# One chunk instead of two by seven products in the last third of a gated MLP, and a last chunk that issues its matmuls ahead of its additions and stores

## The chip, the core and the metric

The kernel runs on one core of one Trainium2 chip. The metric is the device time of one execution in microseconds (us). Five engines work side by side, each in the order of its own instruction list: TensorE (PE, matmuls; its weight loads, PEld, overlap them), VectorE (DVE), ScalarE (ACT), GpSimd (POOL) and SyncE (SP, which here issues the transfers). Matmuls add up in PSUM banks of 128 partitions by 512 fp32 numbers.

## What is computed

One hybrid decoder layer on 256 tokens of width 2048: a norm, one input projection into attention heads and a pooling mixer, an output projection, and then the part that matters here, a gated MLP with a residual:

```python
def conv_ffn(h, w_up, conv_w, conv_b, w_down):
    u = h @ w_up
    ...
    gate, val = jnp.split(y, 2, axis=-1)
    return (jax.nn.silu(gate) * val) @ w_down
...
x = x + conv_ffn(rms_norm(x, ffn_norm_g[l]), w_up[l], conv_w[l], conv_b[l], w_down[l])
```

The hidden width is 5632, that is 44 blocks of 128 rows of `w_down`. All is fp32.

## The kernel before

**Three matmuls for one product.** Each fp32 operand is split into a rounded high part and a low part. A product of two operands is then high·high + low·high + high·low: three matmuls (`triple`, lines 703–706, and the loops over `((0, 0), (1, 0), (0, 1))`). For the weights ScalarE makes the high part `wh` (line 124) and VectorE the low part `wl` (line 129), both 128x1024.

**Units and chunks.** The whole weight stream is cut into units of 128x1024; two units are one chunk, loaded by one 1024 KB transfer into one of four `raw` buffers (line 105). A buffer is given back and the load of the chunk four later issued when the low part of the chunk's second unit has been made (`release`, lines 160–164). There are seven `wh` and six `wl` buffers.

**The order.** A list `steps` holds one entry per unit; the loop in lines 830–853 walks it. In turn `u` it writes the split of units `u+6` (high) and `u+5` (low), the matmuls of unit `u`, and whatever was hung onto that step. So the order of every engine's list comes from this loop; an engine that waits holds all that stands behind it.

**The last product.** The hidden width is worked off in three thirds of 8, 8 and 6 block pairs (`THIRDS`, line 57). Each third first makes its hidden activations (`gate`, `value`) and then multiplies them with its rows of `w_down` in two passes, `down_pair(bp, ...)` with `bp` 0 and 1, one for each half of the 2048 output columns. A pass over a third has as many chunks as block pairs. The output of a pass lies in four PSUM banks, `bank(t, b)`: token tile `t` (128 tokens) by column half `b` (512); the two banks of one `t` are one tile, `ps_down`.

A chunk is a 2x2 block of weights against a 2x2 block of activations (two row blocks by two column halves, two row blocks by two token tiles):

- The plain form (`quad`, lines 744–752) makes eight block products, 24 matmuls, 12 for each unit.
- The form by seven products (`quad_sums`, lines 727–742) makes 21 matmuls, 12 for the first unit and 9 for the second. It needs sums of activations (`token_sums`, lines 690–701, on GpSimd, ScalarE, VectorE) and sums of weights: `seven_sums` (lines 139–145) writes on VectorE a 128x512 low part (line 150) and three subtractions (lines 143–145), and `seven_high`/`seven_low` a further 128x1024 part `s4` (lines 148 and 157).

`MIXED` (line 58) says which chunks of a third take the form by seven: `8: (0, 4)` for the first two thirds, `6: (0, 3)` for the last. Three of the seven products gather in PSUM tiles of their own (`ps_p`, in code `aux`, `p5`, `p7`). When the last chunk of that form in a pass is through, five pieces of work, `add_part(0)` to `add_part(4)`, add these to the residual `x2` (lines 769–783): pieces 0 and 2 are a copy by ScalarE (line 774) and a VectorE addition in PSUM (line 775), pieces 1, 3 and 4 VectorE additions of 128x1024 into `x2` (lines 777, 780, 783). They are hung onto the steps by

```python
s_end = 2 * mixed[-1] + 1
rest = 2 * nq - 1 - s_end
...
if at == s_end + 1 + n * (rest - 1) // 5:
```

With six chunks and `(0, 3)` that gives the steps 8, 8, 9, 9 and 10 of a pass's 12 (0 to 11).

**The end of a pass.** After the last step `close` (lines 785–791) adds the four banks to `x2`, 128x1024 for each `t`, and stores it if this is the last third. The very last pass has no `close`: its last chunk goes through `last_quad` (lines 754–767). For each bank in turn, the last one in two halves of 256 columns, it issues the chunk's six matmuls, then the addition to `x2` (line 766), then the store (line 767).

Of the kernel before, what the change touches and what calls it, by code (L numbers as in the profile page):

```python
# [28 lines left out]
OP = mybir.AluOpType  # L29
# [5 lines left out]
NT = S // P  # L35
# [19 lines left out]
OK = (0, 2, 4, 6, 12, 14, 8, 10)  # L55
V_TILES = [((k, 0), (k, 1)) for k in range(KT - 2)] + [((KT - 2, b), (KT - 1, b)) for b in range(2)]
THIRDS = ((0, 8), (8, 16), (16, 22))
MIXED = {8: (0, 4), 6: (0, 3)}


def bucket(n):
# [9 lines left out]
def layer(ctx: ExitStack, tc: tile.TileContext, xT, xtok, wts, par, rel_d, ident_d, icnt_d, out):  # L71
    nc = tc.nc
# [24 lines left out]
    raws, wparts, shift, late = {}, {}, {}, {}  # L97
# [444 lines left out]
    def after(u, f):  # L542

        hooks.append((u, f))
# [22 lines left out]
    for b in range(2):  # L567
# [4 lines left out]
        for j in range(4):  # L572
            h, u = 4 * b + j, at + 2 * j
# [134 lines left out]
    def down_pair(bp, nq, final):  # L708


        box, runs, mixed = {}, [], MIXED[nq]
        s_end = 2 * mixed[-1] + 1
        rest = 2 * nq - 1 - s_end

        def hid(k, t):
            return [late["hid"][:, k, a, t * P:(t + 1) * P] for a in range(2)]
# [4 lines left out]
        def bank(t, b):  # L721
            return box["tok"][t][:, b, :]

        def part(w, c):
            return [p[:, 512 * c:512 * (c + 1)] for p in w]
# [27 lines left out]

        def last_quad(us, j):
            ws = [wparts.pop(u) for u in us]
            for t in range(NT):
                for b in range(2):
                    cs = (slice(0, 512),) if t * b == 0 else (slice(0, 256), slice(256, 512))
                    for c in cs:
                        for h, w in enumerate(ws):  # L760
                            w = [p[:, c] for p in part(w, b if h == 0 else 1 - b)]
                            for n, (a, i) in enumerate(((0, 0), (1, 0), (0, 1))):
                                nc.tensor.matmul(bank(t, b)[:, c], hid(2 * j + h, t)[a], w[i], start=False,  # L763
                                                 stop=(h == 1 and n == 2), skip_group_check=True)
                        x2 = late["x2"][:, t, (2 * bp + b) * 512:(2 * bp + b + 1) * 512][:, c]
                        nc.vector.tensor_tensor(x2, bank(t, b)[:, c], x2, op=OP.add)
                        nc.sync.dma_start(out[:, t, (2 * bp + b) * 512:(2 * bp + b + 1) * 512][:, c], x2)

        def add_part(n):
            x2 = late["x2"][:, :, 1024 * bp:1024 * (bp + 1)]  # L770
# [23 lines left out]
        for j in range(nq):  # L794
            for h in range(2):
                at = 2 * j + h

                def run(u, j=j, h=h, at=at):
                    if j in mixed:
                        quad_sums(u, j, h)  # L800
                    elif end and j == nq - 1:
                        if h == 1:
                            last_quad((u - 1, u), j)
                    else:
                        quad(u, j, h)
                run.seven = j in mixed and h == 0
                acts = [run]
                for n in range(5):
                    if at == s_end + 1 + n * (rest - 1) // 5:
                        acts.append(lambda n=n: add_part(n))  # L810
                if at == 2 * nq - 1 and not end:
                    acts.append(lambda: close(0))
                runs.append(acts)
        return runs

    for n, (g0, g1) in enumerate(THIRDS):
        after(len(steps), lambda nq=g1 - g0: late.__setitem__("mixed", MIXED[nq]))
        for g in range(g0, g1):
# [7 lines left out]
    n = len(steps)  # L826
# [94 lines left out]
```

## Time and profile before

| | |
|---|---|
| median of 3 runs | 1027.93 us (1027.73 to 1028.13) |
| the profiled execution's own time | 1027.94 us |
| its span, first to last instruction | 1025.8 us |
| TensorE busy | 1015.5 us, 99% of the span |
| VectorE busy | 771.5 us, 75% |
| ScalarE busy | 545.9 us, 53% |

Busy time is summed over the span. A row of the timeline gives the start, the time, the engine, the line, what is written and read and how many were merged, and in brackets how long the engine had been idle and who ended that. A row of the chain of waits is a piece of the chain that ended last. A row of a window gives the length of the window and the busy time of each engine in it with its count of instructions.

### The profile page before, as it was taken

What the parts mean: (1) busy time and instruction counts of PE and PEld (TensorE: products, weight loads), DVE (VectorE), ACT (ScalarE), POOL (GpSimd) and SP (SyncE); (2) the same over time, 40 slices, a digit from 0 to 9 for tenths busy, and PEclk for the clock granted to TensorE, in tenths of its full rate; (3) what the DMA queues carried; (4) which work ended last, traced back from release to release, by engine and by line L of the source; (5) the groups of instructions that cost most, each with busy time, mean ns of one, the idle gap of its engine ahead of it and who ended that gap; (6) DMA issues with size and microseconds to landing.
All of it is one profiled execution on the core that took longest, in us unless ns stands there. A gap on an engine that the chain in (4) does not pass through costs nothing.

```text
span 1025.8 us, 13519 instructions
## 1 busy us (share of the span) xinstructions
PE 1015.5 (99%) x5280; PEld 869.7 (85%) x5280; DVE 771.5 (75%) x968; ACT 545.9 (53%) x734; POOL 63.4 (6%) x78
## 2 busy tenths in 40 slices
PE   9999999999999999999999999999999999999987
PEld 8888888888888888888888888888888888888776
DVE  6966667874667877878977687777898767778994
ACT  6744554565445655555644455555554446555650
POOL 0420005600000000000000000000000000000000
PEclk9999999999999999999999999999999999999999
DMA  9775454485454564454565364554465644545451
GB/s 334 273 279 176 172 169 161 165 306 186 164 205 149 200 215 176 165 195 183 207 241 200 124 234 177 207 186 182 165 246 187 224 165 164 211 180 185 172 197 41
DMA packets 30607, 199.18 MB, mean 194 GB/s; under 512 B 3576, under 2 KB 4472, under 8 KB 7760
## 3 DMA queue, kind: packets, MB, share of 16 engines
q1 hardware_dynamic: 29968, 196.89, 52.9%
q0 software_dynamic: 576, 1.44, 0.6%
q8 instruction: 41, 0.67, 0.3%
q14 instruction: 22, 0.18, 0.0%
HBM read 195.83 MB, written 2.49 MB: 193 GB/s over the span
## 4 chain that ended last, share of the span: by engine, by line
PE 96%; DVE 3%; issue 1%; ACT 0%; DVEq 0%; ACTq 0%
PE ps_feat L185 34%; PE ps_feat L187 17%; PE ps_tok L172 17%; PE ps_down L750 14%; PE ps_v L179 4%; PE ps_p L706 3%; PE ps_down L706 2%; DVE wl L129 1%; PE ps_down L763 1%; PE ps_pool L194 1%; PE ps_s L400 1%; PE ps_start L247 0%; PE ps_T L387 0%; PE ps_x2T L615 0%; PE ps_av L433 0%
## 5 line engine op out<-in xcount | busy, mean ns | idle before, releaser
L129 DVE TENSOR_TENSOR wl<-raw,wh 128x1024 fp32r<-128x1024 f32 x358 | 435.7, 1252 | 75.5 <-PE ps_tok L172 27.7
L185 PE MATMUL ps_feat<-x2h,wh 128*128 128x512 f32 x1408 | 488.6, 392 | 0.0
L124 ACT ACTIVATE wh<-raw 128x1024 fp32r<-128x1024 f32 x358 | 361.7, 1051 | 159.1 <-DVE raw L143 54.5
L187 PE MATMUL ps_feat<-x2h,wl 128*128 128x256 f32 x1408 | 393.6, 280 | 0.0
L185 PEld LDWEIGHTS ps_feat<-x2h,wh 128*128 128x128 f32 x1408 | 264.3, 188 | 58.4
L187 PEld LDWEIGHTS ps_feat<-x2h,wl 128*128 128x128 f32 x1408 | 264.3, 188 | 0.1
L750 PE MATMUL ps_down<-wh,hid 128*128 128x512 f32 x496 | 122.5, 389 | 0.0
L750 PEld LDWEIGHTS ps_down<-wh,hid 128*128 128x128 f32 x496 | 93.1, 188 | 19.3
L667 ACT ACTIVATE y<-u,pv 128x256 f32<-128x256 f32 x88 | 48.2, 594 | 71.5 <-DVE u L662 71.5
L172 PE MATMUL ps_tok<-wh,xh 128*128 128x512 f32 x256 | 70.1, 396 | 0.0
L172 PE MATMUL ps_tok<-wh,cat 128*128 128x512 f32 x256 | 68.8, 390 | 0.0
L750 PE MATMUL ps_down<-wl,hid 128*128 128x512 f32 x248 | 66.3, 389 | 0.0
L668 DVE SCALAR_TENSOR_TENSOR y<-u,pv,y 128x256 f32<-128x256 f32 x88 | 42.4, 482 | 29.6 <-ACT y L667 29.6
L450 DVE TENSOR_TENSOR fs<-ps_feat,fs 128x512 f32<-128x512 f32 x44 | 30.4, 690 | 36.0 <-ACT fs L449 35.9
L172 PEld LDWEIGHTS ps_tok<-wh,cat 128*128 128x128 f32 x256 | 47.6, 188 | 9.6
L172 PEld LDWEIGHTS ps_tok<-wh,xh 128*128 128x128 f32 x256 | 47.5, 188 | 9.5
L750 PEld LDWEIGHTS ps_down<-wl,hid 128*128 128x128 f32 x248 | 46.6, 188 | 9.7
L699 POOL TENSOR_TENSOR s<-y 128x128 f32<-128x128 f32 x12 | 7.3, 612 | 693.9 <-DVE y L684 693.9
L449 ACT ACTIVATE fs<-ps_feat 128x512 f32<-128x512 f32 x44 | 26.1, 594 | 41.6 <-PE ps_feat L187 41.4
L185 PE MATMUL ps_feat<-xh,wh 128*128 128x512 f32 x128 | 46.2, 402 | 0.0
L670 DVE SCALAR_TENSOR_TENSOR y<-u,pv,y 128x256 f32<-128x256 f32 x88 | 42.7, 485 | 3.1
L685 ACT ACTIVATE hid<-y 128x512 fp32r<-128x512 f32 x22 | 13.9, 634 | 49.0 <-DVE y L684 49.0
(168 smaller groups left out, 939.6 us busy)
## 6 DMA issues: line engine op xcount, KB each, us to landing
raw<-in_wts SPq DMA_DIRECT2D x177, 1024.0 KB, 5.0
raw<-in_wts SPq DMA_DIRECT2D x4, 512.0 KB, 7.6
x<-in_xtok SPq DMA_DIRECT2D x1, 2048.0 KB, 9.5
raw<-in_wts SPq DMA_DIRECT2D x7, 256.0 KB, 5.8
xboth<-in_xT SPq DMA_DIRECT2D x4, 256.0 KB, 6.7
T<-band POOLq DMA_DIRECT2D x8, 128.0 KB, 5.4
out<-x SPq DMA_DIRECT2D x2, 512.0 KB, 2.9
out<-x SPq DMA_DIRECT2D x3, 256.0 KB, 2.0
```

The costliest lines, as they stand in the source:

```text
L124: nc.scalar.activation(wparts[u][0], raw(u - 1 if u - 1 in seven else u + 1 if u in seven else u), AF.Copy)
L129: nc.vector.tensor_tensor(wl, raw(u - 1 if u - 1 in seven else u + 1 if u in seven else u), wh.bitcast(F32), op=OP.subtract)
L172: nc.tensor.matmul(ps[:, t, :], act[:, k0 + k, a, t * P:(t + 1) * P], w[:, k * 512:(k + 1) * 512], start=(first and k == 0 and n == 0), st ...
L179: nc.tensor.matmul(ps[:, t, :], act[:, k, a, t * P:(t + 1) * P], w[i], start=(first and n == 0), stop=(last and n == 2))
L185: nc.tensor.matmul(ps, wh[:, ws], act[:, k, :, :], start=(first and n == 0), stop=False, skip_group_check=True)
L187: nc.tensor.matmul(ps[:, S:], wl[:, ws], act[:, k, 0, :], start=False, stop=(last and n == len(ks) - 1), skip_group_check=True)
L450: nc.vector.tensor_tensor(dst, ps[:, :, :S], dst, op=OP.add)
L667: nc.scalar.activation(y[:, m, :], u[:, m, 2:], AF.Identity, scale=cw[2], bias=col(C_CB + f))
L668: nc.vector.scalar_tensor_tensor(y[:, m, :], u[:, m, 1:1 + S], cw[1], y[:, m, :], op0=OP.mult, op1=OP.add)
L670: nc.vector.scalar_tensor_tensor(y[:, m, :], u[:, m, :S], cw[0], y[:, m, :], op0=OP.mult, op1=OP.add)
L706: nc.tensor.matmul(ps, act[a], w[i], start=(first and n == 0), stop=(last and n == 2), skip_group_check=skip)
L750: nc.tensor.matmul(bank(t, b), hid(2 * j + h, t)[a], part(w, b if h == 0 else 1 - b)[i], start=(t == b == 1 and j == 1 and h == 0 and n == ...
```

## The change

`MIXED` takes chunk 3 of the last third out, so that in each of its two passes chunk 0 alone goes by seven products and the chunks 1 to 5 in the plain form. By the rule for `add_part` above the five pieces then stand at the steps 2, 3, 5, 7 and 9 of each pass. The call of `token_sums` for block pair 3 of the last third falls away with it. `last_quad` makes a list of its five pieces, issues the matmuls of all of them and after that the five additions, each with its store.

```diff
-MIXED = {8: (0, 4), 6: (0, 3)}
+MIXED = {8: (0, 4), 6: (0,)}
...
         def last_quad(us, j):
             ws = [wparts.pop(u) for u in us]
-            for t in range(NT):
-                for b in range(2):
-                    cs = (slice(0, 512),) if t * b == 0 else (slice(0, 256), slice(256, 512))
-                    for c in cs:
-                        for h, w in enumerate(ws):
-                            w = [p[:, c] for p in part(w, b if h == 0 else 1 - b)]
-                            for n, (a, i) in enumerate(((0, 0), (1, 0), (0, 1))):
-                                nc.tensor.matmul(bank(t, b)[:, c], hid(2 * j + h, t)[a], w[i], start=False,
-                                                 stop=(h == 1 and n == 2), skip_group_check=True)
-                        x2 = late["x2"][:, t, (2 * bp + b) * 512:(2 * bp + b + 1) * 512][:, c]
-                        nc.vector.tensor_tensor(x2, bank(t, b)[:, c], x2, op=OP.add)
-                        nc.sync.dma_start(out[:, t, (2 * bp + b) * 512:(2 * bp + b + 1) * 512][:, c], x2)
+            pieces = [(t, b, slice(0, 512)) for t, b in ((0, 0), (0, 1), (1, 0))]
+            pieces += [(1, 1, slice(c, c + 256)) for c in (0, 256)]
+            for t, b, c in pieces:
+                for h, w in enumerate(ws):
+                    w = [p[:, c] for p in part(w, b if h == 0 else 1 - b)]
+                    for n, (a, i) in enumerate(((0, 0), (1, 0), (0, 1))):
+                        nc.tensor.matmul(bank(t, b)[:, c], hid(2 * j + h, t)[a], w[i], start=False,
+                                         stop=(h == 1 and n == 2), skip_group_check=True)
+            for t, b, c in pieces:
+                cols_ = slice((2 * bp + b) * 512 + c.start, (2 * bp + b) * 512 + c.stop)
+                x2 = late["x2"][:, t, cols_]
+                nc.vector.tensor_tensor(x2, bank(t, b)[:, c], x2, op=OP.add)
+                nc.sync.dma_start(out[:, t, cols_], x2)
```

**VectorE, from the seven-product sums of the last pass's first chunk to the end of pass 0.** In these rows `wl` is a low part of a unit, `ps_p` a PSUM tile of the seven products, `x2` the residual, `ps_down` the banks that `close` empties. Before, the `add_part` pieces stand together right ahead of `close`:

```order
L129 TENSOR_TENSOR wl_8225<-raw_8096,wh_8220 128x1024 [waits PE_49,Activation_49]
L775 TENSOR_TENSOR ps_p_8075<-ps_p_8075,s_8239 128x512 [waits Activation_49]
L777 TENSOR_TENSOR x2_1868<-ps_p_8075,x2_1868 128x1024 [waits DVE_49]
L129 TENSOR_TENSOR wl_8245<-raw_8138,wh_8222 128x1024 [waits DMAHW5_49,PE_49]
L157 TENSOR_TENSOR s1024l_1874<-raw_8096,s1024h_1873 128x1024
L775 TENSOR_TENSOR ps_p_8075<-ps_p_8075,s_8262 128x512 [waits DVE_49,Activation_49]
L780 TENSOR_TENSOR x2_1868<-ps_p_8075,x2_1868 128x1024 [waits DVE_49]
L129 TENSOR_TENSOR wl_8268<-raw_8138,wh_8243 128x1024 [waits PE_49]
L783 TENSOR_TENSOR x2_1868<-ps_p5_8076,x2_1868 128x2x512 [waits DVE_49]
L129 TENSOR_TENSOR wl_8287<-raw_8156,wh_8266 128x1024 [waits DMAHW6_49,PE_49,Activation_49]
L788 TENSOR_TENSOR x2_1868<-ps_down_8078,x2_1868 128x1024 [waits DVE_49,PE_49]
```

The same stretch after the change (its lines 766 and up stand one lower in the file, so that 780 is 781 and 788 is 789):

```order
L145 TENSOR_TENSOR raw_8089<-raw_8089 128x512 [waits DVE_49]
L781 TENSOR_TENSOR x2_1868<-ps_p_8068,x2_1868 128x1024
L129 TENSOR_TENSOR wl_8222<-raw_8089,wh_8204 128x1024 [waits PE_49,Activation_49]
L129 TENSOR_TENSOR wl_8238<-raw_8108,wh_8219 128x1024 [waits DMAHW5_49,PE_49,Activation_49]
L157 TENSOR_TENSOR s1024l_1874<-raw_8089,s1024h_1873 128x1024 [waits Activation_49]
L784 TENSOR_TENSOR x2_1868<-ps_p5_8069,x2_1868 128x2x512 [waits DVE_49]
L129 TENSOR_TENSOR wl_8258<-raw_8108,wh_8236 128x1024 [waits PE_49,Activation_49]
L129 TENSOR_TENSOR wl_8276<-raw_8146,wh_8256 128x1024 [waits DMAHW6_49,PE_49,Activation_49]
L789 TENSOR_TENSOR x2_1868<-ps_down_8071,x2_1868 128x1024 [waits DVE_49,PE_49]
```

Pieces 0, 1 and 2 have left this stretch for an earlier place in the pass; pieces 3 and 4 stand between the splits, and two splits stand between the last piece and the first row of `close`.

**TensorE at the very end.** `ps_down_8308` and `ps_down_8309` are the tiles of token tile 0 and 1 before; after the change they are `ps_down_8297` and `ps_down_8298`. Before, from the second bank of token tile 0 on:

```order
L763 MATMUL ps_down_8308<-wh_8378,hid_7059 128x512 [waits DVE_49]
L763 MATMUL ps_down_8308<-wh_8378,hid_7059 128x512
L763 MATMUL ps_down_8308<-wl_8396,hid_7059 128x512
L763 MATMUL ps_down_8308<-wh_8394,hid_7059 128x512 x2
L763 MATMUL ps_down_8308<-wl_8422,hid_7059 128x512
L763 MATMUL ps_down_8309<-wh_8378,hid_7059 128x512 x2
L763 MATMUL ps_down_8309<-wl_8396,hid_7059 128x512
L763 MATMUL ps_down_8309<-wh_8394,hid_7059 128x512 x2
L763 MATMUL ps_down_8309<-wl_8422,hid_7059 128x512
L763 MATMUL ps_down_8309<-wh_8378,hid_7059 128x256 [waits DVE_49]
```

The same place after the change:

```order
L762 MATMUL ps_down_8297<-wh_8364,hid_7059 128x512 x2
L762 MATMUL ps_down_8297<-wl_8382,hid_7059 128x512
L762 MATMUL ps_down_8297<-wh_8380,hid_7059 128x512 x2
L762 MATMUL ps_down_8297<-wl_8399,hid_7059 128x512
L762 MATMUL ps_down_8298<-wh_8364,hid_7059 128x512 x2
L762 MATMUL ps_down_8298<-wl_8382,hid_7059 128x512
L762 MATMUL ps_down_8298<-wh_8380,hid_7059 128x512 x2
L762 MATMUL ps_down_8298<-wl_8399,hid_7059 128x512
L762 MATMUL ps_down_8298<-wh_8364,hid_7059 128x256 x2
```

Before, TensorE waits for VectorE ahead of the second bank of a tile and ahead of the last 256 columns; now nothing stands on it there.

**VectorE at the very end.** The five additions before, with the last `add_part` piece ahead of them:

```order
L783 TENSOR_TENSOR x2_1868<-ps_p5_8306,x2_1868 128x2x512 [waits DVE_49,PE_49]
L766 TENSOR_TENSOR x2_1868<-ps_down_8308,x2_1868 128x512 [waits PE_49]
L766 TENSOR_TENSOR x2_1868<-ps_down_8308,x2_1868 128x512 [waits DVE_49,PE_49]
L766 TENSOR_TENSOR x2_1868<-ps_down_8309,x2_1868 128x512 [waits PE_49]
L766 TENSOR_TENSOR x2_1868<-ps_down_8309,x2_1868 128x256 [waits PE_49] x2
```

And after the change:

```order
L784 TENSOR_TENSOR x2_1868<-ps_p5_8295,x2_1868 128x2x512 [waits DVE_49]
L767 TENSOR_TENSOR x2_1868<-ps_down_8297,x2_1868 128x512 [waits PE_49]
L767 TENSOR_TENSOR x2_1868<-ps_down_8297,x2_1868 128x512 [waits DVE_49]
L767 TENSOR_TENSOR x2_1868<-ps_down_8298,x2_1868 128x512 [waits PE_49]
L767 TENSOR_TENSOR x2_1868<-ps_down_8298,x2_1868 128x256 x2
```

They wait for TensorE once for each tile instead of once for each bank or half: the first addition of a tile carries the wait, and the further ones of that tile have none of their own.

## The prediction

> **What bounds the kernel now.** The page first. Its rows say that TensorE is busy nearly all the time and that its clock is never held back:
>
> ```profile
> span 1025.8 us, 13519 instructions
> PE 1015.5 (99%) x5280; PEld 869.7 (85%) x5280; DVE 771.5 (75%) x968; ACT 545.9 (53%) x734; POOL 63.4 (6%) x78
> PEclk9999999999999999999999999999999999999999
> ```
>
> So time can only come from matmuls left out or from the few gaps. The waits of TensorE, next, put names to the gaps; but for the start-up (L244) they all lie in the last 60 us:
>
> ```profile
> PE ps_down L763 <- DVE x L766: 2.1, 3, 0.8
> PE ps_p L706 <- DVE x L780: 1.3, 1, 1.3
> PE ps_down L706 <- DVE x L788: 1.2, 1, 1.2
> PE ps_start L247 <- DVE ones L244: 1.1, 1, 1.1
> PE ps_p L706 <- DVE s1024l L157: 1.1, 1, 1.1
> ```
>
> All four name VectorE. The windows of this stage show that it is the bound there, 7.97 of 8 us while TensorE has 5.85, and that this is over when pass 1 is under way (after the window's length stand the busy times of PE, PEld, DVE, ACT and POOL with their counts, the granted clock, the busy share of the transfer engines and GB/s):
>
> ```profile
> 982.00:990.00 8.00, 5.85 (x24) 3.97 (x22) 7.97 (x8) 2.73 (x4) 0.00 (x0) 1.00 0.61 206
> 998.00:1006.00 8.00, 8.00 (x37) 6.60 (x37) 6.31 (x7) 4.12 (x5) 0.00 (x0) 1.00 0.00 0
> ```
>
> Then TensorE's timeline through both passes of the last third, where each step can be measured from start to start:
>
> ```profile
> 956.35 1.98 PE L750 MATMUL ps_down<-wh,hid 128*128 128x512 f32 x8
> ...
> 967.23 0.62 PE L706 MATMUL ps_p<-s512h,hid 128*128 128x512 f32 x2
> ...
> 973.61 1.98 PE L750 MATMUL ps_down<-wh,hid 128*128 128x512 f32 x8
> ...
> 985.98 0.69 PE L706 MATMUL ps_p<-s512h,hid 128*128 128x512 f32 x2 [1.33 <-DVE x L780]
> ...
> 990.42 0.73 PE L706 MATMUL ps_down<-wh,sx 128*128 128x512 f32 x2 [1.24 <-DVE x L788]
> ...
> 992.60 1.98 PE L750 MATMUL ps_down<-wh,hid 128*128 128x512 f32 x8
> ...
> 1013.68 0.61 PE L763 MATMUL ps_down<-wh,hid 128*128 128x512 f32 x2
> ```
>
> From 956.35 to 967.23 run four plain units, 48 matmuls: 10.88 us, 0.2267 us each, 2.72 a unit of 12. That pace gives what each piece loses. Chunk 3 of pass 0, by seven: 973.61 - 967.23 = 6.38 for 21 matmuls worth 4.76, lost 1.62. Its four plain units after that should end at 973.61 + 10.88 = 984.49, and pass 1 starts at 985.98: lost 1.49. Pass 1's first unit: 985.98 to 990.42 is 4.44 for 2.72, lost 1.72; the nine matmuls to 992.60 take 2.18 for 2.04, lost 0.14. In all 4.97 us. From 992.60 to 1013.68, 93 matmuls in 21.08 us, nothing is lost. The tail comes from the chain:
>
> ```profile
> 1015.24 0.70 DVE x L766
> ...
> 1015.99 3.04 PE ps_down L763 x12
> ...
> 1019.05 0.70 DVE x L766
> ...
> 1020.81 0.44 DVE x L766
> ...
> 1022.31 0.42 DVE x L766
> ```
>
> Additions and matmuls take turns there, so every addition is on the path.
>
> **The change, part by part.** The sum is made against the profiled execution, 1027.94 us (span 1025.8 and 2.1 around it); the median is 1027.93, so no correction is needed.
>
> *More matmuls.* Chunk 3 goes from 21 to 24 in two passes: 6 x 0.2267 = +1.36 us, all on the path. The Trainium skill, "TensorE: Matmul & The Clock Gate", section "Back-to-back issue gap", gives about 131 ns for a 512-column matmul in a sustained stream with weight loads; by that figure the six would be 0.8 us. The rows above measure 226.7 ns in this very stream, so the sum keeps 1.36.
>
> *VectorE in pass 0.* Its list, from the first weight split after the hidden activations to `close`:
>
> ```profile
> 960.68 2.36 DVE L129 TENSOR_TENSOR wl<-raw,wh 128x1024 fp32r<-128x1024 f32 x2
> 962.96 0.69 DVE L150 TENSOR_TENSOR s512l<-raw,s512h 128x512 fp32r<-128x512 f32 x1
> ...
> 966.27 2.35 DVE L129 TENSOR_TENSOR wl<-raw,wh 128x1024 fp32r<-128x1024 f32 x2
> 968.54 1.22 DVE L157 TENSOR_TENSOR s1024l<-raw,s1024h 128x1024 fp32r<-128x1024 f32 x1
> ...
> 979.75 0.70 DVE L775 TENSOR_TENSOR ps_p<-ps_p,s 128x512 f32<-128x512 f32 x1 [1.00 <-ACT s L774]
> 980.48 1.22 DVE L777 TENSOR_TENSOR x<-ps_p,x 128x1024 f32<-128x1024 f32 x1
> 981.62 1.22 DVE L129 TENSOR_TENSOR wl<-raw,wh 128x1024 fp32r<-128x1024 f32 x1
> ...
> 989.15 2.35 DVE L788 TENSOR_TENSOR x<-ps_down,x 128x1024 f32<-128x1024 f32 x2
> ```
>
> From start to start a 128x1024 operation takes 1.14 us (980.48 to 981.62, and half of 966.27 to 968.54), a 128x512 in PSUM 0.73 (979.75 to 980.48), the four sums L150 and L143 to L145 together 966.27 - 962.96 = 3.31. One chunk by seven so costs VectorE 3.31 + 1.14 = 4.45 us extra. Check on before: 12 splits 13.68, two chunks by seven (chunk 3 and pass 1's first) 8.90, `add_part` 2 x 0.73 + 3 x 1.14 = 4.88, the 1.00 of waiting: 28.46, and 960.68 + 28.46 = 989.14; the trace has `close` at 989.15. Now take out one chunk by seven and the wait for ScalarE (its copies for `add_part` can be made in the middle of the pass, since the seven products end at 956.35): 28.46 - 4.45 - 1.00 = 23.01, so VectorE reaches `close` at 983.69.
>
> *TensorE meets it.* From 956.35 ten plain units run, 27.20 us, to 983.55. `close` can therefore start at about 983.7, frees token tile 0 at 984.83 and tile 1 at 985.97. Pass 1 writes its first 12 matmuls into the `ps_p` tiles, which the last `add_part` piece left two splits ahead of `close`, about 981.4; the first bank of tile 0 is written at 983.55 + 2.72 = 986.27, tile 1 six matmuls on at 987.63. Both are free by 1.4 us or more. So all 4.97 us go, hidden by VectorE's place in pass 0; without that cover each us that VectorE is later than 1.4 comes back one for one. What each addition now held early waits for, ScalarE's copy, holds the splits behind it; those are wanted by TensorE five units, 13.6 us, later. In pass 1 VectorE loses 4.45 us of work as well, where TensorE lost nothing: no gain. The dropped `token_sums` (GpSimd, ScalarE, VectorE) lay beside a full TensorE: none either. Main part: 1.36 - 4.97 = -3.61; the last chunk starts at 1010.07 in place of 1013.68.
>
> *The tail.* Two starts 0.35 us and three matmuls apart give the pace of the 256-column ones, 0.117 us:
>
> ```profile
> 1021.64 0.28 PE L763 MATMUL ps_down<-wl,hid 128*128 128x256 f32 x1
> ...
> 1021.99 0.28 PE L763 MATMUL ps_down<-wl,hid 128*128 128x256 f32 x1
> ```
>
> Without waits the last matmul starts 18 x 0.2267 + 11 x 0.117 = 5.37 us after the chunk's first, and VectorE, as before (1021.99 to 1022.31), 0.32 later: 5.69, against 1022.31 - 1013.68 = 8.63. That is -2.94. In exchange the additions of token tile 1 pile up behind the last matmul, since all three wait for it: 0.73 + 0.45 + 0.42 = 1.60 in place of 0.42, +1.18. The two of tile 0 wait for the twelfth matmul only and are done before. Tail: -1.76.
>
> *The stores.* The last three now leave within 0.9 us of each other. They are 256, 128 and 128 KB:
>
> ```profile
> out<-x SPq DMA_DIRECT2D x3, 256.0 KB, 2.0
> ...
> out<-x SPq DMA_DIRECT2D x2, 128.0 KB, 1.7
> ```
>
> Nothing shows such stores together. At the least nothing changes; if the bytes queue, 128 KB cost 0.3 us (2.0 - 1.7), so the last lands up to 0.3 later. I take 0, the bytes being few, and keep 0.3 for the range.
>
> Sum: 1027.94 - 3.61 - 1.76 = **1022.6 us**.
>
> **The rivals.**
>
> *Part of the border stays.* My VectorE walk takes it to be never held up between 960.7 and 983.7. One stall like the 1.00 us above fits into the 1.4 of slack; two do not. Up to 1.5 us would come back: 1022.6 to 1024.1. Against it: the walk met `close` within 0.01 us for before.
>
> *The border stays whole.* If what held TensorE at 985.98 and 990.42 were not the amount of VectorE's work but the order (a piece or `close` always behind a split that waits for TensorE), 4.97 would stay: 1027.6, no change. For it: `close` still stands behind two splits. Against: those splits wait for units 9 and 10 of the pass, which TensorE ends before unit 11.
>
> *The stores serialise.* The Trainium skill, "DMA: Bandwidth & Descriptors", section "Latency and other measured facts", has HBM access at 0.2 us on average and 2 us at high load; that speaks against sending the last stores together. By the rows: one after the other they take 2.0 + 1.7 + 1.7 = 5.4 us from the first issue, against 0.9 + 1.7 = 2.6 in my sum: +2.8, 1025.4 us. Against it are weight loads, eight times as large, which land in 5.0 us next to each other:
>
> ```profile
> raw<-in_wts SPq DMA_DIRECT2D x177, 1024.0 KB, 5.0
> ```
>
> *Slower: the weights become the bound.* With VectorE out of the way TensorE takes a 1024 KB chunk each 5.44 us, 193 GB/s, and a load leaves only when VectorE gives its buffer back. To end over 1030.0 us TensorE would have to lose 7.4 us over the 64 us of these passes, 11%: that is so if loads run below 173 GB/s in the stage, say by waiting behind the pass's 512 KB stores; at 170 it would be 1031.3 (64.2 x 193 / 170 = 72.9 us, 8.7 more). Against it: the window above moved 206 GB/s there, with the transfer engines 0.61 busy.
>
> That the matmuls of the last chunk still wait is ruled out by TensorE's list, which has no wait at these places.
>
> **How the numbers follow.** A measurement of this kernel can tell about 0.2% (2.06 us) from no change. All gaps gone, 1022.6 with stores up to 0.3: 0.82. Part of the border: 0.09. Stores in series: 0.03. The border whole: 0.04. Weights: 0.02. The first three are faster, 0.94; the fourth is no change; the last is slower. The range starts 0.6 under the forecast (the medians' spread of 0.2 on either side, and 0.4 for ends of matmuls that are modelled and additions that may follow each other closer than their own times) and reaches up over the stores' 0.3 and most of the partial border: 1022.0 to 1024.1.
>
> **What would show it.** Right: no TensorE wait in the last third; pass 0's end and pass 1's first unit without a gap, `close` starting within 1.4 us of the first unit of pass 1; 24 matmuls of the last chunk in 5.7 us; three additions, one after the other, behind the last matmul; last store out about 1.6 us after it. Wrong: a wait of L706 for `close` or for an `add_part` piece (VectorE still late), weight splits idle on a transfer, or more than 3.4 us from the last addition to the end of the span where it is 3.1 now (1022.73 to 1025.8).

## The result and the profile after

| | before | after |
|---|---|---|
| median, us | 1028.03 (1027.73 to 1028.46, 6 runs) | 1022.66 (1022.27 to 1023.09, 6 runs) |
| ratio to before | | 0.9948, 95% interval 0.9935 to 0.9961 |
| profiled execution, us | 1027.94, span 1025.8 | 1022.76, span 1021.0 |

The changed kernel is 5.37 us faster by the medians; 1022.6 was forecast. First the page's two lines of the changed kernel and all that its view of TensorE's waits holds:

```profile
span 1021.0 us, 13504 instructions
PE 1015.0 (99%) x5286; PEld 871.4 (85%) x5286; DVE 761.6 (75%) x957; ACT 542.7 (53%) x729; POOL 61.4 (6%) x74
```

```profile
PE ps_start L247 <- DVE ones L244: 1.1, 1, 1.1
```

Six matmuls more, eleven VectorE instructions less, and of the waits only the one at the start of the program is left. The chain that ended last now runs through TensorE alone from the first pass of the last third to the last matmul:

```profile
956.82 27.20 PE ps_down L750 x120
984.02 2.72 PE ps_p L706 x12
986.74 2.04 PE ps_down L706 x9
988.78 21.76 PE ps_down L750 x96
1010.54 5.52 PE ps_down L762 x30
1016.06 0.02 issue
1016.09 0.69 DVE x L767
1016.78 0.33 DVEq L918
1017.11 0.33 DVE x L767
```

Ten plain units in 27.20 us, then 2.72 and 2.04 for the two units by seven products, without a gap at the border of the passes; 3.35 us had been lost there before, and 1.62 in chunk 3. At the end stand one addition of 512 columns and, back to back, two of 256; they take 1.35 us together. (The row of DVEq L918 covers the time of the first of those two: VectorE's own timeline has both between 1016.70 and 1017.44.)

VectorE is still full around the border. The first row is the window of 8 us that was shown of before (PE 5.85 then), the others VectorE's and TensorE's rows there:

```profile
982.00:990.00 8.00, 8.00 (x37) 6.60 (x37) 7.95 (x8) 3.67 (x4) 0.00 (x0) 1.00 0.92 352
```

```profile
981.34 2.35 DVE L129 TENSOR_TENSOR wl<-raw,wh 128x1024 fp32r<-128x1024 f32 x2
983.61 2.36 DVE L789 TENSOR_TENSOR x<-ps_down,x 128x1024 f32<-128x1024 f32 x2
```

```profile
986.58 0.62 PE L706 MATMUL ps_down<-wh,sx 128*128 128x512 f32 x2
```

`close` starts at 983.61 and frees the first tile 1.14 us later, at 984.75; TensorE writes that tile at 986.58. So VectorE is not idle, it is early: 1.8 us of slack.

### The profile page after: what moved, and what is told of

The parts are those of the page before. It is cut to its first block, busy times and chain, and to the rows that moved or that the text cites. A ratio compares the mean times of both kernels' runs of the same rounds, so it can differ in the third digit from the quotient of the medians.

```text
span 1021.0 us, 13504 instructions
## 1 busy us (share of the span) xinstructions
PE 1015.0 (99%) x5286; PEld 871.4 (85%) x5286; DVE 761.6 (75%) x957; ACT 542.7 (53%) x729; POOL 61.4 (6%) x74
## 4 chain that ended last, share of the span: by engine, by line
PE 99%; DVE 0%; DVEq 0%; issue 0%
PE ps_feat L185 34%; PE ps_feat L187 18%; PE ps_down L750 18%; PE ps_tok L172 17%; PE ps_v L179 4%; PE ps_p L706 3%; PE ps_down L706 2%; PE ps_pool L194 1%; PE ps_down L762 1%; PE ps_s L400 1%; PE ps_start L247 0%; PE ps_x2T L615 0%; PE ps_T L387 0%; PE ps_av L433 0%; PE ps_eT L422 0%; PE ps_av L434 0%
## 5 line engine op out<-in xcount | busy, mean ns | idle before, releaser
L750 PE MATMUL ps_down<-wh,hid 128*128 128x512 f32 x528 | 130.4, 390 | 0.0
L750 PEld LDWEIGHTS ps_down<-wh,hid 128*128 128x128 f32 x528 | 99.2, 188 | 20.5
L750 PE MATMUL ps_down<-wl,hid 128*128 128x512 f32 x264 | 70.6, 390 | 0.0
L750 PEld LDWEIGHTS ps_down<-wl,hid 128*128 128x128 f32 x264 | 49.6, 188 | 10.3
```

The lines of the kernel that those rows point to most:

```text
L750: nc.tensor.matmul(bank(t, b), hid(2 * j + h, t)[a], part(w, b if h == 0 else 1 - b)[i], start=(t == b == 1 and j == 1 and h == 0 and n == ...
```

## The experiments

Theory by amount: a second chunk by seven gave VectorE more work in pass 0 than fitted between the hidden activations and `close`; that held TensorE, and the rest of the gain is the tail. Against it stood a theory by the tail (all of the gain comes from the last chunk, and the six matmuls are a loss) and one by order (it was the `add_part` pieces standing right ahead of `close`). Times are medians, each taken on one chip beside the kernel before. There were three such groups: both parts alone, the late pieces and the kernel with room behind the border stood beside 1028.04 us for the kernel before, one and four doubled parts and the first two tails beside 1028.29, the rest beside 1028.52. So a difference of a few tenths between groups is read from the ratios. The rows carry each kernel's own line numbers, from line 754 on a few off those of before (with doubled parts one more from line 129 on).

**Each part alone.** The chunks alone, `last_quad` as before:

```diff
-MIXED = {8: (0, 4), 6: (0, 3)}
+MIXED = {8: (0, 4), 6: (0,)}
```

> The change of the chunks alone, the last chunk as before. Amount theory (the second chunk by seven overloaded VectorE in pass 0, and that held TensorE for 4.97 us): 3.6 us under the kernel before, about 1024.4, and no TensorE wait but the three of the last chunk. Tail theory (the gain comes from the last chunk, the six more matmuls are a loss): 1.4 over the kernel before, about 1029.4.

And the new `last_quad` alone, `MIXED` left at `6: (0, 3)`:

> The last chunk alone, with two chunks by seven in each pass as before. Amount theory: the border's waits stay as they were (1.1, 1.3 and 1.2 us), only the tail shrinks: 1.3 to 1.8 us under the kernel before, 1026.2 to 1026.7. Tail theory: all of the 5.4 us and the 1.4 of the matmuls that are not added, about 1021.3.

Measured beside 1028.04 for the kernel before: the chunks alone 1024.31 us (ratio 0.9961, 0.9949 to 0.9974), the tail alone 1026.30 (0.9983, 0.9974 to 0.9992). TensorE's waits with the chunks alone:

```profile
PE ps_down L763 <- DVE x L766: 2.1, 3, 0.8
PE ps_start L247 <- DVE ones L244: 1.1, 1, 1.1
```

and with the tail alone:

```profile
PE ps_p L706 <- DVE x L781: 1.4, 1, 1.4
PE ps_down L706 <- DVE x L789: 1.2, 1, 1.2
PE ps_start L247 <- DVE ones L244: 1.1, 1, 1.1
PE ps_p L706 <- DVE s1024l L157: 1.1, 1, 1.1
```

Each part takes its own waits away and leaves the other's. 3.73 and 1.74 us make 5.47, against 5.37 for both: the parts add up, and the tail theory is out.

**Amount or order.** The changed kernel with the `add_part` pieces put back to late steps:

```diff
-                    if at == s_end + 1 + n * (rest - 1) // 5:
+                    if at == (8 + n * 3 // 5 if final else s_end + 1 + n * (rest - 1) // 5):
```

> The changed kernel with the five add_part pieces back at the steps 8, 8, 9, 9 and 10 of a pass. Amount theory: VectorE's work in pass 0 is the same, it only comes to close about 1.4 us later (one stall on the six wl buffers), inside the 1.8 us of slack: within 0.5 us of the changed kernel, about 1022.7. Order theory (it is the pieces standing right ahead of close that hold TensorE): most of the 4.97 us come back, 1026 to 1027.6, with TensorE waiting for a piece or for close at the border.

It took 1023.92 us (0.9959, 0.9946 to 0.9971): 1.26 over the changed kernel, where at most 0.5 was expected, and far from the 3.3 to 4.9 of the order theory. VectorE's rows in pass 0 show two stalls, and TensorE's row the wait that follows:

```profile
970.26 1.22 DVE L129 TENSOR_TENSOR wl<-raw,wh 128x1024 fp32r<-128x1024 f32 x1 [1.50 <-PE ps_down L750]
...
976.94 0.70 DVE L776 TENSOR_TENSOR ps_p<-ps_p,s 128x512 f32<-128x512 f32 x1 [0.99 <-ACT s L775]
...
986.35 2.35 DVE L789 TENSOR_TENSOR x<-ps_down,x 128x1024 f32<-128x1024 f32 x2
```

```profile
987.62 0.73 PE L706 MATMUL ps_down<-wh,sx 128*128 128x512 f32 x2 [1.13 <-DVE x L789]
```

With no piece between them the splits run ahead until the six `wl` buffers are full (1.50), and a piece placed late finds ScalarE behind on its copy (0.99). I had counted the first and not the second: 2.5 us together, more than the slack of 1.8, and `close` at 986.35 is too late. So the early steps are worth 1.3 us of the gain. That the amount carries the rest is what the next runs test.

**More work for VectorE and nothing else.** In the changed kernel the low parts of some units of pass 0 are computed twice (`units` holds their numbers within the pass):

```diff
-        nc.vector.tensor_tensor(wl, raw(u - 1 if u - 1 in seven else u + 1 if u in seven else u), wh.bitcast(F32),
-                                op=OP.subtract)
+        for _ in range(2 if u - 2 * wts.shape[0] + 24 in units else 1):
+            nc.vector.tensor_tensor(wl, raw(u - 1 if u - 1 in seven else u + 1 if u in seven else u), wh.bitcast(F32),
+                                    op=OP.subtract)
```

One unit:

> As the kernel with four doubled low parts, but only one (unit 9): 1.14 us more on VectorE. Amount theory with its slack of 1.8 us: nothing, 1022.7, no TensorE wait at the border. If VectorE's work reached the end one for one: 1023.8.

Two, with the changed kernel once more beside it as a base:

> The changed kernel with two low parts of pass 0 (units 9 and 10) computed twice: 2.3 to 2.5 us more on VectorE, 0.5 to 0.7 beyond the slack of 1.8. Amount theory, one for one beyond the slack: TensorE waits 0.5 to 0.7 us for close, and with the 0.3 that a restart costs the time is 0.8 to 1.0 over the changed kernel, clock unbroken. If the clock falls after any wait of TensorE: 2 us or more over it.

> The changed kernel once more, as the base for the kernels beside it on this chip. All theories: 0.994 to 0.996 of the kernel before, about 1022.7.

Three:

> As before with three low parts (units 9 to 11): 3.4 to 3.8 us on VectorE, 1.6 to 2.0 beyond the slack, a wait like those of the kernel before the change or a little longer (it had 1.3). One for one with a restart: 1.9 to 2.3 over the changed kernel, each run alike. If the clock can fall after a wait this long, as it did after 2.4 us with four doubled parts: runs spread over 1 us or more, their slow ones with a mean clock under 0.999.

Four:

> The changed kernel with the low parts of four units of pass 0 of the last third (units 8 to 11 of the pass) computed twice: four more VectorE operations of 128x1024, 4.55 us, about what a second chunk by seven costs VectorE, with no other change. Amount theory: close frees the first tile 4.55 us later, 2.7 us past the 1.8 us of slack that the changed kernel's trace shows (984.75 to 986.58), so TensorE waits 2.7 us for close and the time is about 1025.4. If the amount of VectorE work is not the cause: 1022.7.

| doubled | median, us | range | ratio to before, interval | longest TensorE wait for `close` |
|---|---|---|---|---|
| none (again) | 1022.96 | 1022.71 to 1023.12 | 0.9947, 0.9934 to 0.9959 | none |
| 1 | 1023.12 | 1022.44 to 1023.27 | 0.9947, 0.9935 to 0.9960 | none |
| 2 | 1023.42 | 1023.04 to 1023.59 | 0.9951, 0.9937 to 0.9964 | 0.69 |
| 3 | 1025.71 | 1024.41 to 1026.95 | 0.9973, 0.9962 to 0.9985 | 1.96 |
| 4 | 1027.55 | 1025.66 to 1029.30 | 0.9990, 0.9981 to 0.9999 | 2.37 |

In the traces a doubled part takes 1.26 us of VectorE more, so that one, two, three and four make 1.27, 2.53, 3.79 and 5.05 us. One costs nothing. With two, TensorE waits 0.69 us for `close`, as 2.53 less the slack of 1.83 has it, and the 21 matmuls around it lose 1.0; by the medians the kernel is 0.46 us over the changed one beside it, where 0.8 to 1.0 was expected. So the slack is between 1.3 and 2.5 us, as the trace had it (1.8). With four, 0.6 us more VectorE work than a second chunk by seven (5.05 for 4.45), nearly all of the gain is gone with no other edit. So the amount of VectorE's work in pass 0 is enough by itself to hold TensorE.

But three and four cost more than one for one (1025.4 was expected for four), and their runs spread. The windows of the kernel with three doubled parts, around its wait, and TensorE's row:

```profile
986.00:988.00 2.00, 0.62 (x3) 0.19 (x1) 2.00 (x3) 1.06 (x1) 0.00 (x0) 1.00 0.99 410
988.00:990.00 2.00, 1.41 (x4) 1.18 (x5) 2.00 (x3) 0.00 (x0) 0.00 (x0) 0.75 1.05 360
990.00:992.00 2.00, 2.00 (x6) 1.52 (x6) 2.00 (x3) 1.20 (x2) 0.00 (x0) 0.50 0.96 365
992.00:994.00 2.00, 2.00 (x10) 1.62 (x9) 1.68 (x2) 0.35 (x1) 0.00 (x0) 0.90 0.68 277
```

```profile
988.59 0.90 PE L707 MATMUL ps_down<-wh,sx 128*128 128x512 f32 x2 [1.96 <-DVE x L790]
```

The seventh number, behind POOL's, is the granted clock: around a stretch of 1.96 us without a matmul it is halved for about 3.4 us (0.75, 0.50 and 0.90 over three windows are 1.0, 2.0 and 0.4 us at half clock), and in the middle window six matmuls run where ten or eleven do at full clock. In windows of half a microsecond the clock is still 1.00 through the wait and falls at about 989.0, 0.4 us after TensorE has started again; with four doubled parts it falls at about 990.0, 0.4 us before the restart at 990.39. Of the 3.8 us lost at this border (the 21 matmuls from 983.74 to 992.27 take 8.53 us for 4.76) 2.0 is the wait and 1.7 the halved clock; the restart makes up the little that is left.

It doesn't fall in every run. One execution of each kernel was profiled; for the others only the mean clock tells, and 1.7 us lost in 1024 bring it to 0.998 or less. That is so in 3 of the 6 runs with three parts and 8 of the 11 with four, and in no run of any other kernel here. With three parts the runs with 0.999 or 1.000 took 1024.41 to 1024.98 us, those with 0.998 1026.43 to 1026.95; with four, 0.999 went with 1025.66 to 1026.69 and 0.996 with 1029.30. The runs without the fall are one for one: with three parts 1.5 to 2.0 over the changed kernel beside them, for 3.79 less 1.83; with four 3.0 to 4.0 over the changed kernel, for 5.05 less 1.83. The Trainium skill, "TensorE: Matmul & The Clock Gate", section "HAM oscillation — how this bites in real kernels", has a clock halved after gaps of more than about 3.4 us; here 2.0 was enough, and the 1.33 us of the kernel before was not.

**Room behind the border.** Pass 1 keeps its second chunk by seven, pass 0 has one:

```diff
-        box, runs, mixed = {}, [], MIXED[nq]
+        box, runs, mixed = {}, [], (0,) if final and bp == 0 else MIXED[nq]
```

with `MIXED` at `6: (0, 3)`.

> The changed kernel, but pass 1 of the last third keeps its second chunk by seven (chunks 0 and 3), with its add_part pieces at 8, 8, 9, 9 and 10 there; pass 0 has chunk 0 alone. Amount theory: behind the border VectorE has room for 4.45 us more, so three matmuls go for nothing: 0.7 us under the changed kernel, about 1022.0, with no TensorE wait. If a chunk by seven costs TensorE time wherever it stands: 1 to 2 us over the changed kernel, about 1024.

1022.21 us (0.9941, 0.9927 to 0.9954), 0.45 under the changed kernel by the medians, which noise of a few tenths leaves likely rather than sure; the chain has the three matmuls less and no wait in pass 1, and `token_sums` for block pair 3 stands in this kernel again:

```profile
988.91 10.88 PE ps_down L750 x48
999.79 2.72 PE ps_p L706 x12
1002.51 2.04 PE ps_down L706 x9
1004.55 5.44 PE ps_down L750 x24
1010.00 5.52 PE ps_down L762 x30
```

From 988.91 to 1010.00 it takes 21.09 us, where the changed kernel's same stretch took 21.76. A chunk by seven does save 0.67 us, where VectorE has room for it, and its `token_sums` cost nothing.

**The tail.** The last chunk in another order: the first bank of token tile 1 first, with its addition and store, then tile 0, then the last bank:

```diff
-            pieces = [(t, b, slice(0, 512)) for t, b in ((0, 0), (0, 1), (1, 0))]
-            pieces += [(1, 1, slice(c, c + 256)) for c in (0, 256)]
+            for pieces in (((1, 0, 0, 512),), ((0, 0, 0, 512), (0, 1, 0, 512)), ((1, 1, 0, 256), (1, 1, 256, 512))):
+                for t, b, c0, c1 in pieces:
+                    for h, w in enumerate(ws):
...
+                for t, b, c0, c1 in pieces:
...
+                    nc.vector.tensor_tensor(x2, bank(t, b)[:, c0:c1], x2, op=OP.add)
+                    nc.sync.dma_start(out[:, t, cols_], x2)
```

> The changed kernel with the last chunk in another order: the first bank of token tile 1 first with its addition and store, then both banks of tile 0 with theirs, then the two halves of the last bank. TensorE's only wait there is for an addition made some 2 us earlier. Theory of the tail (additions piled up behind the last matmul, and three stores close together that each land 0.3 later): two additions in place of three behind the last matmul, 0.6 us less, and up to 0.3 from the stores: 1021.8 to 1022.1, span 1020.1 to 1020.4. If neither the pile nor the stores are on the path: 1022.7.

Then both edits:

> Both: pass 1 with chunks 0 and 3 by seven, pass 0 with chunk 0 alone, and the last chunk with the first bank of token tile 1 first. Sum of the two parts, 0.5 measured and 0.6 to 0.9 forecast, under the changed kernel: 1021.2 to 1021.6. If the additions of the add_part pieces, late in pass 1 here, hold the last chunk's additions: no better than 1022.2.

And both, with one store on ScalarE's queue:

> The fastest kernel so far (pass 1 with chunks 0 and 3 by seven, the first bank of token tile 1 first) with the store of the first half of the last bank issued by ScalarE's queue in place of SyncE's. If SyncE, busy with one store for 0.33 to 0.41 us, holds the next: 0.1 to 0.3 less, 1021.0. If the two stores get in each other's way behind the queue: no change, 1021.3.

The order alone took 1021.89 us (0.9937, 0.9925 to 0.9950), both edits 1021.30 (0.9929, 0.9917 to 0.9942), the second queue 1020.95 beside a slower chip (0.9928, 0.9916 to 0.9941). The end of the chain with both edits:

```profile
1009.87 5.52 PE ps_down L761 x30
1015.40 0.02 issue
1015.42 0.42 DVE x L766
1015.85 0.33 DVEq L917
```

Two additions, 0.76 us, in place of three, 1.35: that gain is there. The time from the last addition to the end of the span was 3.07 us before (1022.73 to 1025.8), 3.56 in the changed kernel (1017.44 to 1021.0), 3.32 with both edits (1016.18 to 1019.5) and 3.31 with the second queue (1015.59 to 1018.9). The second queue gained nothing: the ratio is the same, and the 0.6 us between the two profiled executions already stand ahead of the last third (by the chain its first plain unit starts at 956.25 for 956.83). The last store left at once there, and took 2.0 us to land for 1.9. With both edits the kernel is 6.99 us under the kernel before on its chip (1028.29); but for the second queue, which can't be told from it, no other here is faster.

## Why the prediction was right, step by step

- *Border, 4.97 us lost and given back by VectorE's amount.* Right. The walk put `close` at 983.69, the trace has 983.61, though the pass began 0.31 later in that execution (its first plain unit at 956.66 for 956.35): there was a little less work than counted (the two additions in PSUM took 0.60 and 0.61 from start to start, 964.35 to 964.95 and 969.48 to 970.09, for 0.73), and the slack was 1.8 us, not 1.4. The rows with doubled parts show that it was the amount; the late pieces show that their early steps were needed as well, which the walk only had as a remark (one stall fits, two do not).
- *Six matmuls, 1.36 us on the path.* Right: the stretch from the first plain unit to the last chunk is 53.72 us (956.66 to 1010.38), as reckoned.
- *Tail, matmuls.* Right: 5.71 us from the last chunk's first matmul to the first addition behind it (1010.38 to 1016.09), 5.69 forecast.
- *Tail, additions and stores.* Two sizes were off, against each other. The three additions took 1.35 us for 1.60, because two of 256 columns back to back take 0.33 each and not 0.45. The stores cost 0.49 (3.56 against 3.07), for 0 taken and 0.3 as the end of the range. The rows of the stores now say:

```profile
out<-x SPq DMA_DIRECT2D x3, 256.0 KB, 2.2
...
out<-x SPq DMA_DIRECT2D x2, 128.0 KB, 2.0
```

  That 2.0 is the middle of 2.1 and 1.9. The last store took 1.9 us to land where it took 1.7 before: 0.2. The other 0.3 lies ahead of it, since it was issued at 1017.72, 0.28 after its addition, where before it followed at once (1022.76 for 1022.73). The prediction had reckoned with a later landing and not with a later issue, and named more than 3.4 us to the end of the span as a sign that it is wrong: that sign came, at 3.56. Stores in series (2.8 more) are ruled out even so.
- *The sum.* In the trace: 0.31 later into the pass, -3.61, -2.92, +0.93 for the additions, +0.49 for the stores, -4.80 in all, which is the difference of the spans. The profiled times differ by 5.18, since 1.76 us lie around the span now and 2.14 before. The span came out 0.57 above the 1020.43 that the terms of the prediction give. The prediction had left the 2.1 us around the span unchanged; that they shrank by 0.38 was luck, and with it the 1022.66 by the median is closer than the terms were.
- *Not foreseen.* "Each us that VectorE is later than 1.4 comes back one for one" held for the waits up to 1.1 us; with waits of 1.96 us and more the clock took its share in 11 of 17 runs.

Open: why 0.4 us less lie outside the span. The chunks alone show it (1024.25 us for a span of 1022.5) and so does the tail alone (1025.97 for 1024.1), so it can't be put down to either part; no run tells more.

## What to carry to other kernels

A form that saves TensorE work and costs VectorE work pays only where VectorE has room: walk the other engine's list from its last forced start to the point where TensorE needs it, and put the form in the passes that leave room. Auxiliary work belongs early in the stage, where a stall has slack to die in; the same pieces placed late cost 1.3 us here. Where two banks share one tile, the order of the banks decides who waits for whom: let the tile that is closed last be started first.

## What the runs showed of the hardware that was not expected

A wait of TensorE of 1.33 us left its granted clock at 1.00; around one of 1.96 us or 2.37 us it went to 0.50 for about 3.4 us in the profiled executions, and by the mean clock in 11 of 17 executions in all; with three doubled parts the executions so lie 2.5 us apart. And three stores issued within 0.9 us (1016.81 to 1017.72), 512 KB together, landed only 0.2 to 0.4 us later each than the same stores spaced out (2.2 for 2.0, 2.1 and 1.9 for 1.7 us), while the two of 512 KB at the border, where 352 GB/s were moved in that window, took a median of 6.2 us to land for 2.9 before, with nobody waiting for them:

```profile
out<-x SPq DMA_DIRECT2D x2, 512.0 KB, 6.2
```
